# A re-planned two-layer kernel: gate row by products, a quarter scaled on ScalarE, early setups, and other distances in the planner

## The chip, the cores and the metric

One core of a Trainium2 chip runs the whole program in one launch. The metric is the device time of one execution in microseconds (us); the median of 3 runs of the kernel before is 3489.16 us (3485.51 to 3496.49). Inside the core, TensorE (PE, with its weight loads PEld), VectorE (DVE), ScalarE (ACT) and GpSimd (POOL) compute, and SyncE (SP) issues every transfer.

## What is computed

Two layers on x of 2048 rows by 1024 columns, in float32. The first layer begins with three rows of 1024 numbers, and the third of these, `gate`, is used only at the layer's end:

```
c_act = silu(c)
shift, scale, gate = split(c_act @ ada_w + ada_b, 3)      # ada_w: 1024 x 3072
h = rmsnorm(x, g_pre) * (1 + scale) + shift
proj = h @ w_in                                           # then three mixers: window attention, rwkv, gla
y = concat(attn, rwkv, gla) @ w_out
x = x + gate * rmsnorm(y, g_post)
```

The second layer normalizes x again, projects it, picks the 256 best keys of each query by a small index product, attends to them, adds a pooled branch, and merges both by gates. It needs cosines and sines of the positions, which depend on no other result.

## The kernel before

**Stages.** The 2048 rows are worked in four quarters of 512. For each quarter, `build_h` (line 792) loads rows, normalizes and transposes them, scales them into the array `raw`, and splits `raw` into a high and a low part (float32r), since each dense product is taken as three float32r products of parts (`mm3`). `dense` then runs the projections; the weights of a tile are split once by `weights` (line 895), stored as two parts of 512 KB each in an internal DRAM tensor (`scr_w`), and later loaded from there, again 512 KB a part, into a ring of two buffers for each part. Then come the mixers, the first output product, the second layer's projections, the search for the best keys and the attention, and the second output (`out2`).

**The start.** `body` (line 2209) records `setup`, the early rows of quarter 0, `ada` (shift and scale), `split_early`, the first dense tiles of quarter 0, `build_h` of quarter 1, `ada_gate` (line 771), `setup2` (line 1696: cosines and sines, and some scaled columns), `pool_setup` (line 2084: a few constants by 64 one-column MEMSETs on VectorE), then `proj1_setup`, whose product `d_wx` three of the tiles need. `ada_gate` makes the row `gate` in two halves (j = 4 and 5). For each half `ada_rows` (line 760) loads eight pieces of 128x512 of `ada_w` and accumulates them on VectorE, one TENSOR_SCALAR and seven SCALAR_TENSOR_TENSOR; one product with a column of ones then adds over the partitions. The scratch row `d_grow` receives the result. The loads rotate through eight buffers.

**Scaling.** For quarter q the letter `BX[q]` (line 37) says where `build_h` applies scale and shift to the 16 transposed pieces of 128x256 that lie in PSUM: "d" records a TENSOR_SCALAR on VectorE, "a" an ACTIVATE Identity on ScalarE. The splitting copy that follows is ScalarE's either way, and the subtraction GpSimd's.

**The order of the work.** No instruction is issued when it is written. Every operation is first recorded with its dependencies and a price from a formula (`price`, line 567), and `order` (line 381) plans the whole program: `forward` (line 312) walks through time and gives each engine, whenever it is free, the ready operation of the highest rank; `backward` (line 352) computes new ranks from the plan's end; and so on for up to `PASSES` = 32 passes, ending earlier after 12 without a better plan. The plan with the lowest planned total is emitted (`emit`, line 408; so all instructions carry line 414), and each engine then runs its own list in that order, waiting at each instruction for what it needs. Three things of the planner matter here:

- Operations that may run elsewhere (`others`, line 496) have several ways: copies and scalings by a constant or a column can go to VectorE, ScalarE, and in part GpSimd. A TENSOR_SCALAR with scale and shift, both columns, has no other way; an ACTIVATE Identity with a bias may also become one on VectorE.
- `lag` (line 610) is the time between the end of one operation and the start of one that depends on it. For whatever a transfer is followed by, a load, a store that frees a buffer, or a store that a load reads back, it is 900 ns. The transfer itself is planned as an issue, 1125 ns, and its bytes at 360 per ns in one queue.
- `until` (line 291) makes VectorE and GpSimd exclude each other in the plan. A VectorE operation takes part if `port` (line 545) says so: those with two tensors in SBUF do. Copies and scalings of one tensor don't.

```
    def until(self, o, e, t):
        if e == "vector" and o.port:
            return max(t, self.held["gpsimd"] - 60.0)
        if e == "gpsimd":
            return max(t, self.held["vector"] - 60.0)
        return t
```

Of the kernel before, what the change touches and what calls it, by code (L numbers as in the profile page):

```python
# [8 lines left out]
F32 = mybir.dt.float32  # L9
F32R = mybir.dt.float32r  # L10
# [8 lines left out]
PSUM = bass.MemoryType.PSUM  # L19
# [14 lines left out]
F, S0, S2 = 0, 8, 12  # L34
W1, W2, W3, W4, W5 = 1, 1, 1, 1, 1
P1, P2, P3, P4, P5, P6 = 1, 1, 1, 1, 1, 1
BX, BY = "-dad", "ssss"
EJ = ((2, "vector"), (3, "tensor"), (0, "tensor"), (1, "vector"))
B1, B2, B3, B4, B5 = 1, 1, 1, 1, 1
K0, K1, K2, K3, M0, M1 = 3, 4, 4, 4, 2, 2  # L40
PASSES, PATIENCE = 32, 12
SWITCH, NEAR, LOOK, WAIT, AHEAD = 90.0, 3000.0, 12, 150.0, 60000.0
FLEX, MARGIN, GAIN = 3, -10000.0, 500.0
ENGINES = ("tensor", "vector", "scalar", "gpsimd", "sync")
RW, PHL, GS = 2, 4, 2

# [10 lines left out]


class Op:
    __slots__ = ("eng", "name", "args", "kw", "preds", "succs", "cost", "start", "end", "more", "ways", "kind", "port")  # L60


class Plan:
# [3 lines left out]
    def __init__(self, tc, ctx):  # L67
        self.tc, self.nc = tc, tc.nc
        self.ops = []
        self.memo = {}  # L70
        self.pitch = {}
        self.used = {}
        self.free = [(0, self.SBUF * 4)]
        self.places, self.start = {}, {}
        ps = ctx.enter_context(tc.tile_pool(name="psum", bufs=1, space=PSUM))
        self.banks = [ps.tile([128, 512], F32, name=f"bank{i}") for i in range(8)]
        self.bank_names = {b.name: i for i, b in enumerate(self.banks)}
        self.idle = list(range(8))
        self.rings = {}
        self.junk = ()  # L80
        self.totals = []
        for e in ("tensor", "vector", "scalar", "gpsimd", "sync"):
            setattr(self, e, Engine(self, e))
# [98 lines left out]
    def record(self, eng, name, args, kw):  # L182
        o = Op()
        o.eng, o.name, o.args, o.kw = eng, name, args, kw
        o.preds, o.succs, o.more = {}, [], set()
        i = len(self.ops)
        reads, writes = operands(name, args, kw)
        o.cost = price(eng, name, args, kw, reads, writes)
        o.ways = [(eng, name, args, kw, o.cost)]
        o.kind = kind(name, reads) if eng == "tensor" else None  # L190
        o.port = port(name, reads)
        for way in others(eng, name, args, kw, reads, writes):
            o.ways.append((*way, price(*way, reads, writes)))
        for aps, w in ((reads, False), (writes, True)):
            for ap in aps:
                r = self.region(ap)
                if r is not None:
                    self.touch(o, i, r, w and ap.tensor.name not in self.junk, ap.tensor.name)
        o.preds.pop(i, None)
        self.ops.append(o)  # L200
# [89 lines left out]

    def until(self, o, e, t):

        if e == "vector" and o.port:
            return max(t, self.held["gpsimd"] - 60.0)
        if e == "gpsimd":
            return max(t, self.held["vector"] - 60.0)
        return t
# [14 lines left out]
    def forward(self, rank, goal):  # L312

        ops = self.ops
        end, seq, dma = [0.0] * len(ops), [], [0.0]

        def take(i, e, t, now, avail, done):
            o = ops[i]
            free = self.until(o, e, t)
            if len(o.ways) > 1:  # L320
                mine = next(w for w in o.ways if w[0] == e)
                home = o.ways[0][0]
                if e != home:
                    slack = goal - rank[i] - t + MARGIN
                    if slack > 0:
                        return t + slack
                    w = o.ways[0]
                    start = max(now[home], t)
                    start += sum(ops[j].cost for r, j in avail[home] if -r > rank[i] and not done[j])
                    if start + w[4] <= t + mine[4] + GAIN:  # L330
                        return max(start + w[4] - mine[4] - GAIN, t + 50.0)
                o.eng, o.name, o.args, o.kw, o.cost = mine
            o.start = t
            if e == "sync":
                now[e] = t + 475
                dma[0] = o.end = max(dma[0], t + 1125) + o.cost
            else:
                now[e] = o.end = free + o.cost
                if o.port and e in self.held:
                    self.held[e] = o.end  # L340
                if e == "tensor":
                    if o.kind != self.kind:
                        now[e] = o.end = o.end + SWITCH
                    self.kind = o.kind
            end[i] = o.end
            seq.append(i)

        self.walk([len(o.preds) for o in ops],
                  lambda i: [(s, end[i] + lag(ops[i], ops[s], data)) for s, data in ops[i].succs], rank, take)
        return max(end), end, seq  # L350

    def backward(self, end):

        ops = self.ops
        tail, dma = [0.0] * len(ops), [0.0]
        ways = [o.ways for o in ops]
        for o in ops:
            o.ways = [(o.eng, o.name, o.args, o.kw, o.cost)]

        def take(i, e, t, now, avail, done):  # L360
            o = ops[i]
            if e == "sync":
                now[e] = t + 475
                dma[0] = max(dma[0], t) + o.cost
                tail[i] = dma[0] + 1125
            else:
                now[e] = tail[i] = self.until(o, e, t) + o.cost
                if o.port and e in self.held:
                    self.held[e] = tail[i]
                if e == "tensor":  # L370
                    if o.kind != self.kind:
                        now[e] = tail[i] = tail[i] + SWITCH
                    self.kind = o.kind

        self.walk([len(o.succs) for o in ops],
                  lambda i: [(p, tail[i] + lag(ops[p], ops[i], data)) for p, data in ops[i].preds.items()], end, take)
        for o, w in zip(ops, ways):
            o.ways = w
        return tail

    def order(self):

        ops = self.ops
        for i, o in enumerate(ops):
            for j, data in o.preds.items():
                ops[j].succs.append((i, data))
        rank = [0.0] * len(ops)
        for i in reversed(range(len(ops))):
            rank[i] = max((rank[s] + lag(ops[i], ops[s], data) for s, data in ops[i].succs), default=0.0) + ops[i].cost
        best, goal = None, math.inf  # L390
        stale = 0
        for k in range(PASSES):
            total, end, seq = self.forward(rank, goal)
            stale += 1
            if stale > PATIENCE:
                break
            if best is None or total < best[0]:
                stale = 0
                best = total, seq, [(o.eng, o.name, o.args, o.kw, o.cost, o.start, o.end) for o in ops]
            rank = self.backward(end)  # L400
            goal = total
            self.totals.append(total)
        self.total, self.seq, how = best
        for o, h in zip(ops, how):
            o.eng, o.name, o.args, o.kw, o.cost, o.start, o.end = h
        return self.seq
# [135 lines left out]
         "copy_predicated", "tensor_tensor_reduce"}  # L542


def port(name, reads):

    if name not in PAIRS:
        return False
    return all(reads[i].space != PSUM for i in (0, -1 if name == "scalar_tensor_tensor" else 1))


# [8 lines left out]
def width(ap):  # L560
    n = 1
    for d in list(ap.shape)[1:]:
        n *= d
    return n
# [45 lines left out]
def lag(a, b, data):  # L610

    if a.eng == b.eng and not data:
        return 0.0
    if a.eng == "sync":
        return 900.0
    if b.eng == "sync":
        return 100.0
    return LAG[a.eng][b.eng]
# [6 lines left out]
class Kern:  # L625
# [145 lines left out]
    def ada_gate(self):  # L771
        nc, A = self.nc, self.A
        for j in (4, 5):
            acc = self.ada_rows(j)
            p = self.bank("mt", NT)[:1]
            nc.tensor.matmul(p, self.ones1, acc, start=True, stop=True)
            r = self.x0.tile([1, 512], F32, name="adar", bufs=2)
            nc.sync.dma_start(r, dram(A["ada_b"], j * 512, [[0, 1], [1, 512]]))
            g = self.x0.tile([1, 512], F32, name="adag", bufs=2)
# [1429 lines left out]
def body(tc, A):  # L2209
    with ExitStack() as ctx:  # L2210
        K = Kern(tc, A, ctx)
        tc = K.plan
# [12 lines left out]
        with tc.tile_pool(name="c1", bufs=1) as K.c1:  # L2225
            with tc.tile_pool(name="x0", bufs=1, top=True) as K.x0:
# [6 lines left out]
                dense(t1[:M0], "x", (0,))  # L2233
                build("x", 1)
                K.ada_gate()
                K.setup2()
                K.pool_setup()
            K.proj1_setup()
            K.rwkv_setup()
            K.gla_setup()  # L2240
# [95 lines left out]
```

## Time and profile before

| | |
|---|---|
| median of 3 runs | 3489.16 us (3485.51 to 3496.49) |
| the profiled execution: its own time | 3483.89 us |
| its span, first to last instruction | 3482.1 us |
| mean granted TensorE clock, share of full speed | 0.956 |
| instructions | 53683 |
| busy: PE, PEld, DVE, ACT, POOL | 91%, 74%, 69%, 50%, 38% |
| moved by transfers | 631.69 MB, mean 181 GB/s |

The span is the time between the first and the last instruction of the profiled execution; 1.8 us of its own time lie around it. Busy shares are averages over stages with different limits. In rows of waits the columns are the engine, what it waited for, the total in us, the number of waits and the longest. In rows of groups the columns are busy us, mean ns of one, and the idle time before. In rows of the timeline they are the start, the length, the engine and the operation, and in brackets the idle time before and what ended it. "x4" counts instructions, and a float32 product appears as two MATMUL records. The clock column of the windows is the granted TensorE clock as a share of 2.4 GHz, so 0.50 is 1.2 GHz.

### The profile page before, as it was taken

Reading aid. Unit: us, or ns where it says so; the run is one execution under the profiler, and the core shown is the slowest. Engines: PE = TensorE matmul, PEld = TensorE weight load, DVE = VectorE, ACT = ScalarE, POOL = GpSimd, SP = SyncE. Lnnn points to the kernel's source line nnn. Section 1 sums busy time; section 2 is a strip of 40 time slices with the busy share of each in tenths; the row PEclk is TensorE's granted clock in tenths of the full one; section 3 lists DMA queues with packets and bytes.
Section 4 is the critical chain, followed back from the end, with each engine's and each line's share of the span. In section 5 each row is a group of like instructions: output and inputs, shape, how many; then the busy total and the mean of one; then the engine's idle time right before and its main releaser. Section 6 shows DMA issues by size and latency. Waiting matters only on the chain.

```text
span 3482.1 us, 53683 instructions
## 1 busy us (share of the span) xinstructions
PE 3165.3 (91%) x18258; PEld 2567.1 (74%) x18258; DVE 2399.1 (69%) x5421; ACT 1756.7 (50%) x3458; POOL 1336.7 (38%) x1379
## 2 busy tenths in 40 slices
PE   6899988998898999798999999999999988898988
PEld 5677666776666888787887777777777766777877
DVE  6367966666883656258878888789788687775442
ACT  3122225432123454257776767875786957446330
POOL 2232545441333554443323444353132236353421
PEclk7899989999998999999999999999999999899999
DMA  8477467547547888656644344362322346665656
GB/s 273 170 248 209 157 174 229 167 151 214 150 121 232 256 271 296 214 173 216 212 157 137 134 139 140 132 213 91 120 73 90 121 152 230 226 212 163 212 162 220
DMA packets 453961, 631.69 MB, mean 181 GB/s; under 512 B 83751, under 2 KB 309552, under 8 KB 453430
## 3 DMA queue, kind: packets, MB, share of 16 engines
q1 hardware_dynamic: 453686, 628.26, 56.1%
q8 instruction: 143, 2.34, 0.3%
q14 instruction: 132, 1.08, 0.1%
HBM read 397.31 MB, written 230.82 MB: 180 GB/s over the span
## 4 chain that ended last, share of the span: by engine, by line
PE 38%; DMA 13%; DVE 9%; ACT 6%; issue 4%; POOL 3%; SPq 1%; ACTq 0%; DVEq 0%; POOLq 0%
PE bank L414 38%; DVE arena L414 9%; DMA arena<-scr_w 6%; ACT arena L414 6%; POOL arena L414 3%; DMA arena<-in_w_in 1%; DMA arena<-in_w_out 1%; DMA out<-arena 1%; SPq L414 1%; DMA arena<-scr_y 0%; DMA arena<-scr_q 0%; DMA scr_x<-arena 0%; DMA arena<-scr_p_zb 0%; DMA arena<-in_w_branch_b 0%; DMA arena<-scr_yT 0%
## 5 line engine op out<-in xcount | busy, mean ns | idle before, releaser
L414 PE MATMUL bank<-arena 128*128 128x512 f32 (+8 forms) x18258 | 3165.3, 337 | 312.5 <-DVE arena L414 124.4
L414 PEld LDWEIGHTS bank<-arena 128*128 128x128 f32 (+3 forms) x18258 | 2567.1, 181 | 910.4 <-DVE arena L414 225.2
L414 POOL TENSOR_TENSOR arena<-arena 128x512 fp32r<-128x512 f32 (+16 forms) x1116 | 1240.1, 1127 | 1618.8 <-ACT arena L414 975.3
L414 ACT ACTIVATE arena<-arena 128x512 fp32r<-128x512 f32 (+32 forms) x1195 | 966.7, 824 | 804.4 <-DVE arena L414 421.1
L414 ACT ACTIVATE arena<-bank 128x512 f32<-128x512 f32 (+8 forms) x1423 | 724.4, 550 | 797.6 <-PE bank L414 649.9
L414 DVE TENSOR_TENSOR arena<-arena 128x512 fp32r<-128x512 f32 (+27 forms) x822 | 583.4, 724 | 209.3 <-ACT arena L414 103.6
L414 DVE SCALAR_TENSOR_TENSOR arena<-arena 128x512 f32<-128x512 f32 (+10 forms) x661 | 433.8, 661 | 59.5 <-POOL arena L414 19.3
L414 DVE TENSOR_SCALAR arena<-arena 128x1 f32<-128x1 f32 (+6 forms) x1129 | 272.8, 248 | 168.3 <-ACT arena L414 124.9
L414 DVE TENSOR_SCALAR_CACHE_REDUCE arena<-arena 128x384 int8<-128x384 bf16 (+13 forms) x238 | 351.3, 1476 | 11.9 <-ACT arena L414 6.8
L414 DVE CUSTOM_DVE_ANT_0 arena<-bank,arena 128x512 f32<-128x512 f32 (+3 forms) x448 | 251.7, 565 | 62.6 <-PE bank L414 60.6
L414 DVE TENSOR_TENSOR arena<-bank,arena 128x512 f32<-128x512 f32 (+3 forms) x170 | 95.4, 569 | 181.2 <-PE bank L414 144.3
L414 POOL TENSOR_SCALAR arena<-arena 128x4 f32<-128x4 f32 (+10 forms) x169 | 69.0, 409 | 327.9 <-DVE arena L414 159.1
L414 DVE SCALAR_TENSOR_TENSOR arena<-arena,bank 128x512 f32<-128x512 f32 (+1 forms) x264 | 127.5, 487 | 75.6 <-PE bank L414 42.4
L414 DVE COPY arena<-bank 128x512 f32<-128x512 f32 (+8 forms) x146 | 79.6, 548 | 114.9 <-PE bank L414 106.5
L414 ACT ACTIVATE arena<-bank,arena 128x512 f32<-128x512 f32 (+3 forms) x175 | 99.5, 579 | 65.0 <-PE bank L414 64.2
L414 DVE SCALAR_TENSOR_TENSOR arena<-bank,arena 64x64 f32<-64x64 f32 (+4 forms) x209 | 82.0, 393 | 63.1 <-PE bank L414 48.3
L414 ACT ACTIVATION_READ_ACCUMULATOR arena<-arena 128x1 f32 x590 | 114.9, 195 | 0.0
L414 POOL MEMSET arena<- 64x256 f32 (+7 forms) x69 | 21.8, 319 | 109.9 <-PE bank L414 57.6
L414 DVE CAST arena<-arena 128x512 fp32r<-128x512 f32 (+5 forms) x50 | 37.2, 751 | 24.2 <-PE bank L414 6.3
L414 DVE TENSOR_SCALAR arena<-bank 64x256 f32<-64x256 f32 (+2 forms) x44 | 18.0, 410 | 51.4 <-PE bank L414 47.0
L414 DVE TENSOR_TENSOR_SCAN arena<-arena 128x512 f32<-128x512 f32 (+14 forms) x26 | 53.1, 2041 | 0.2
L414 DVE TENSOR_REDUCE arena<-arena 128x1 f32<-128x3 f32 (+6 forms) x148 | 37.3, 252 | 9.5 <-ACT arena L414 8.1
(18 smaller groups left out, 215.7 us busy)
## 6 DMA issues: line engine op xcount, KB each, us to landing
arena<-scr_w SPq DMA_DIRECT2D x340, 512.0 KB
scr_w<-arena SPq DMA_DIRECT2D x174, 512.0 KB
arena<-in_w_in SPq DMA_DIRECT2D x52, 512.0 KB
arena<-in_x SPq DMA_DIRECT2D x32, 512.0 KB
scr_p_g<-arena SPq DMA_DIRECT2D x64, 256.0 KB
arena<-scr_p_g SPq DMA_DIRECT2D x64, 256.0 KB
arena<-in_ada_w SPq DMA_DIRECT2D x48, 256.0 KB
arena<-scr_p SPq DMA_DIRECT2D x16, 532.0 KB
```

Of the source, the lines that this page charges most:

```text
L414: ins = getattr(getattr(self.nc, o.eng), o.name)(*o.args, **o.kw)
```

## The change

1. `ada_gate` no longer accumulates on VectorE. Each half of the gate is a sum of eight products on TensorE, with one column of `cact` as the stationary operand and a loaded piece of 128x512 as the moving one. The loads, the addition of the bias and the product with `norm_post` stay.
2. `BX[1]` becomes "a": quarter 1 is recorded with ACTIVATE Identity.
3. Operations recorded by `setup2` and `pool_setup` are marked early, and each pass adds 60 us to their rank.
4. `lag` after a transfer becomes 2700 ns in place of 900.
5. `port` is asked for each engine, and for VectorE it now also says yes to a TENSOR_SCALAR or copy of float32 from SBUF to SBUF with more than one column and a single output.
6. Up to 200 passes, ending after 30 without a better plan.

```diff
-BX, BY = "-dad", "ssss"
+BX, BY = "-aad", "ssss"
-PASSES, PATIENCE = 32, 12
+PASSES, PATIENCE = 200, 30
+EARLY = 60000.0
...
-        o.port = port(name, reads)
+        o.early = self.early
+        o.port = {e: port(e, name, reads, writes) for e in ("vector", "gpsimd")}
...
-        if e == "vector" and o.port:
+        if e == "vector" and o.port[e]:
...
-                if o.port and e in self.held:
+                if e in self.held and o.port[e]:
...
         for k in range(PASSES):
+            rank = [r + EARLY if o.early else r for r, o in zip(rank, ops)]
             total, end, seq = self.forward(rank, goal)
...
-def port(name, reads):
+def port(eng, name, reads, writes):
     if name not in PAIRS:
-        return False
+        return eng == "vector" and name in ("tensor_scalar", "tensor_copy") and len(writes) == 1 and width(writes[0]) > 1 \
+            and all(x.space != PSUM and x.dtype in (F32, F32R) for x in reads[:1] + writes)
...
     if a.eng == "sync":
-        return 900.0
+        return 2700.0
...
     def ada_gate(self):
         for j in (4, 5):
-            acc = self.ada_rows(j)
             p = self.bank("mt", NT)[:1]
-            nc.tensor.matmul(p, self.ones1, acc, start=True, stop=True)
+            for k in range(8):
+                nc.tensor.matmul(p, self.cact[:, k:k + 1], self.ada_load(j, k, "v"), start=k == 0, stop=k == 7)
...
                 K.ada_gate()
+                tc.early = True
                 K.setup2()
                 K.pool_setup()
+                tc.early = False
```

Since `order` plans all operations together, every one of these edits can move any instruction of the program on any engine's list.

## Rows read from the trace of the kernel before

**Rows 1.** Windows of four stretches: PE, PEld, DVE, ACT, POOL busy, PEclk, DMA share, GB/s.

```profile
0.00:1044.00 1044.00, 927.68 (x4977) 712.11 (x4978) 709.02 (x1534) 309.73 (x692) 384.46 (x360) 0.93 0.61 189
1044.00:1740.00 696.00, 614.57 (x4397) 544.57 (x4397) 412.63 (x1159) 359.77 (x951) 301.45 (x361) 0.94 0.72 234
1740.00:2786.00 1046.00, 1014.02 (x5337) 802.71 (x5336) 853.04 (x1987) 772.21 (x1353) 386.81 (x448) 0.99 0.39 129
2786.00:3482.00 696.00, 608.99 (x3551) 507.69 (x3549) 424.40 (x746) 314.97 (x463) 263.98 (x210) 0.96 0.60 197
```

**Rows 2.** Waits over the whole span, of PE and of the transfers' queue (SPq).

```profile
PE bank L414 <- DVE arena L414: 124.4, 107, 10.1
PE bank L414 <- ACT arena L414: 78.6, 76, 6.1
PE bank L414 <- DMA arena<-scr_w: 73.7, 52, 11.0
...
SPq L414 <- PE bank L414: 900.4, 376, 20.3
```

**Rows 3.** Waits of PE for scr_w, in the four stretches of rows 1.

```profile
PE bank L414 <- DMA arena<-scr_w: 18.2, 12, 4.9
...
PE bank L414 <- DMA arena<-scr_w: 31.6, 15, 11.0
...
PE bank L414 <- DMA arena<-scr_w: 4.7, 7, 1.2
...
PE bank L414 <- DMA arena<-scr_w: 19.2, 18, 2.4
```

**Rows 4.** Windows of the start, columns as in rows 1.

```profile
47.00:60.00 13.00, 3.70 (x10) 2.24 (x11) 12.56 (x16) 5.80 (x10) 9.06 (x6) 0.50 0.85 265
60.00:83.00 23.00, 18.75 (x83) 13.64 (x82) 20.87 (x43) 6.70 (x13) 10.11 (x8) 0.87 0.76 238
83.00:101.00 18.00, 6.81 (x18) 3.28 (x18) 17.40 (x43) 2.78 (x6) 4.32 (x6) 0.50 0.61 201
...
117.00:174.00 57.00, 54.75 (x226) 43.46 (x226) 6.85 (x14) 10.69 (x14) 12.16 (x6) 0.94 0.55 191
```

**Rows 5.** Groups of VectorE by shape, from 47 to 101 us.

```profile
L414 DVE SCALAR_TENSOR_TENSOR arena<-arena 128x512 f32<-128x512 f32 x14 | 10.3, 739 | 0.0
...
L414 DVE TENSOR_SCALAR arena<-bank,arena 128x256 f32<-128x256 f32 x16 | 7.7, 532 | 0.5 <-PE bank L414 0.4
...
L414 DVE SCALAR_TENSOR_TENSOR arena<-arena 128x128 f32<-128x128 f32 x9 | 2.5, 283 | 0.1
```

**Rows 6.** The product with a one-column stationary operand: timeline, and its group to 130 us.

```profile
89.48 1.87 PE L414 MATMUL bank<-arena 128*1 128x512 f32 x2 [5.26 <-DVE arena L414]
...
L414 PE MATMUL bank<-arena 128*1 128x512 f32 x4 | 2.9, 814 | 5.3 <-DVE arena L414 5.3
```

**Rows 7.** Groups of ScalarE over the span: Identity with columns for scale and bias.

```profile
L414 ACT ACTIVATE arena<-bank,arena 128x256 f32<-128x256 f32 x40 | 19.6, 514 | 16.2 <-PE bank L414 16.2
```

**Rows 8.** Loads: a 512 KB one in the timeline, a pair of 512 KB in the chain.

```profile
109.07 0.38 SPq L414 DMA_DIRECT2D arena<-in_w_in  x1
...
113.21 1.06 ACT L414 ACTIVATE arena<-arena 128x1024 fp32r<-128x1024 f32 x1 [3.54 <-DMA arena<-in_w_in]
...
3082.64 7.29 DMA arena<-scr_w
```

**Rows 9.** Timeline of the start: VectorE scalings of 128x1024, and a GpSimd subtraction.

```profile
20.41 1.41 DVE L414 TENSOR_SCALAR arena<-arena 128x1024 f32<-128x1024 f32 x2 [7.43 <-POOL arena L414]
...
51.31 7.09 POOL L414 TENSOR_TENSOR arena<-arena 128x1024 fp32r<-128x1024 f32 x3 [0.68 <-ACT arena L414]
...
54.45 5.41 DVE L414 TENSOR_SCALAR arena<-arena 128x1024 f32<-128x1024 f32 x4
```

**Rows 10.** Timeline: the last MEMSETs of the setups, and the load of the positions.

```profile
12.60 0.38 DVE L414 MEMSET arena<- 128x1 f32 x24
...
44.39 1.65 SPq L414 DMA_DIRECT2D arena<-in_positions  x1
```

More of the change, by code (lines that the diff above doesn't have):

```diff
@@ L59 @@
 class Op:
-    __slots__ = ("eng", "name", "args", "kw", "preds", "succs", "cost", "start", "end", "more", "ways", "kind", "port")
+    __slots__ = ("eng", "name", "args", "kw", "preds", "succs", "cost", "start", "end", "more", "ways", "kind", "port", "early")
 class Plan:
@@ L80, in __init__ @@
         self.junk = ()
+        self.early = False
         self.totals = []
@@ L367, in take @@
                 now[e] = tail[i] = self.until(o, e, t) + o.cost
-                if o.port and e in self.held:
+                if e in self.held and o.port[e]:
                     self.held[e] = tail[i]
```

## The prediction

> **What bounds the kernel.** I read the page's shares first, where TensorE leads with 91%, and then the windows: its busy time is 927.7 + 614.6 + 1014.0 + 609.0 = 3165 us of 3482 [rows 1], so some 317 us are left in which it does nothing, and what the change can win lies in them unless it takes work off TensorE, which it does not. The same windows say where that time is: 116.3 us before 1044, 81.4 to 1740, 32.0 to 2786 and 87.0 in the last stretch [rows 1]. The third stretch has TensorE busy 97% of the time, so the other three carry what can be had. The waits name the causes: TensorE waited 124.4 us for VectorE, 78.6 for ScalarE and 73.7, in 52 waits, for loads of split weights from scr_w [rows 2]. By stretch, those loads are 18.2, 31.6, 4.7 and 19.2 us [rows 3]: few where TensorE has much other work, long where it has not. Last I read the start in finer windows. From 47 to 101 us VectorE is busy 12.56 + 20.87 + 17.40 = 50.8 of 54 us, and TensorE 3.70 + 18.75 + 6.81 = 29.3, with a granted clock of 0.50, its lower level of 1.2 GHz, in the first and the last of these windows, where it had little to do [rows 4]. Here VectorE is the bound. From 117 to 174 us TensorE is busy 54.75 of 57 [rows 4], so what the start saves moves all that follows forward.
>
> **Gate row and second quarter, together.** Both take work off VectorE just in that stretch. The gate's accumulations are 14 SCALAR_TENSOR_TENSOR of 0.739 us, 10.3 us busy [rows 5], and two first TENSOR_SCALARs, which I count at the same price, 1.5 us at most. Quarter 1 has 16 scalings of 0.532 us, 7.7 us busy [rows 5]. VectorE is left with 50.8 - 10.3 - 1.5 - 7.7 = 31.3 us. ScalarE takes the 16 at 0.514 us each [rows 7], 8.2 us; it is busy 15.3 of the 54 us [rows 4], so this lies beside other work, and without that cover it would cost at most the 8.2. The planner may hand an Identity back to VectorE; then VectorE has 39.0 us, which is still below what TensorE needs, so I cost that at nothing.
>
> TensorE pays. One product with a one-column stationary operand took 1.87 us at the lower clock, and the two of them 4 x 0.814 = 3.26 us, so the other took 1.39 [rows 6]. Sixteen come and two go: 14 x 1.39 = 19.5 us at the price of the second, 14 x 1.87 = 26.2 at that of the first, and 14 x 0.94 = 13.1 if all ran at the upper clock and the price is halved with it. TensorE then has 42.4 to 55.5 us of work in a stretch of 54. I take the middle price, since the clock in this stretch is between its levels: 48.8 us, a gain of **5 us**, between 12 and a loss of 1. The loads of the gate stay as they are, in number and in SP's queue; only their reader changes, and a late one now holds up TensorE's list behind it instead of VectorE's.
>
> **Small setups first.** The 64 MEMSETs run by 13 us already [rows 10], when VectorE has nothing else to do. What really moves is the cosine chain, which begins with the load of the positions, issued at 44.39 us [rows 10]: some 25 small operations on VectorE, 9 of which took 0.283 us each [rows 5]; at that price they are 7 us in all. They cost the same wherever they stand; ahead of the scalings that open quarter 0 they would delay these by at most 7 us, and behind them by nothing. I take 0, because VectorE has just been relieved of 19 us there, and keep 0 and 7. One more load goes ahead in SP's queue, 1.65 us by its row [rows 10].
>
> **Loads counted longer.** A 512 KB load is planned as 1.125 + 524288/360000 = 2.58 us, plus 0.9: 3.48 us before, 5.28 after. A pair in one queue is 4.94 before and 6.74 after. In the trace the single load took from 109.07 to 113.21, 4.14 us, and a pair in the last stretch 7.29 [rows 8]. So the plan of before was short by 0.66 and 2.35 us, and the new one is over by 1.14 and short by 0.55. Where the plan is short, TensorE's list reaches a product whose weights aren't there, and stands. Where it is over, the list has other work first and the load is early, which costs nothing on TensorE. The 45 waits outside the third stretch come to 69.0 us, 1.53 each; the 7 inside it, where other products stand ready, to 4.7, or 0.67 each [rows 3]. If the 45 came down to 0.67, that would be 45 x 0.86 = 38.7 us. I take a third of it, **13 us**: an instruction put forward into a gap has inputs too, and TensorE's 203 us of waits for VectorE and ScalarE [rows 2] say that these are often what is late next. The bounds are all 73.7 us, and a loss of 16, an estimate: a fifth of the 78.6 us of waits for ScalarE added by a new order.
>
> The other answer to the same question comes from the Trainium skill. Its page "DMA: Bandwidth & Descriptors", section "Anatomy of one DMA — SWDGE (gpsimd) path", gives, for transfers that GpSimd issues, about 2.0 us fixed plus the bytes at 436 GB/s, which makes an estimate of 3.2 us for 512 KB: by that rule 3.48 was already enough, the load term is 0 and the time 3482 us. The trace speaks against it with 4.14 and 7.29 us.
>
> **Copies exclude GpSimd.** Two VectorE scalings of 128x1024 took 1.41 us without GpSimd at work; four took 5.41 while GpSimd ran a subtraction of 7.09 us in three [rows 9]. That is 2.6 us more than 4 x 0.70, in the stretch that VectorE bounds. Counting this lets the planner put something else there. I take **2 us**; the bounds are 2.6 and a loss of 2.4, one subtraction of 7.09 / 3 that now starts later with a product behind it. Elsewhere VectorE is not the bound.
>
> **More passes.** No row shows what a plan's lower total is worth on the chip; I take 0, and its two sides lie within those of the load term, which is also a matter of order.
>
> **The sum.** 5 + 13 + 2 = 20 us. The profiled execution took 3483.9 us, which gives 3463.9; the median of the runs is 5.3 us above it, so I predict **3469 us** as a median.
>
> **Rivals.**
> - *The load waits are waits for buffers.* The rings hold two buffers for each part, and the transfers' queue stood 900.4 us waiting for TensorE [rows 2]: a load that can't be issued sooner isn't helped by an earlier place. For it: 45 of the 52 waits are in stretches with little else to do. Against: 49.8 us of these waits are in the first and second stretch, where other tiles are open. Only 5 + 2 us are won: 3489 - 7 = 3482 us. Chance 0.12.
> - *The loads were counted long enough.* Then the 0.66 us by which the single load exceeded the plan was chance, and the new distance changes order without effect: again 3482 us. Against it is the pair of 7.29 us. Chance 0.08. The rule of the skill's page above would give this one.
> - *The products fill TensorE at the start* (slower). TensorE has 24.7 us idle from 47 to 101, and at the lower clock the products ask for 26.2. If half of its old waits stay, 12.4 us, because its list is in order and now also stands for pieces of `ada_w`, the stretch takes 29.3 + 26.2 + 12.4 = 67.9 us, 13.9 more than 54. Without a gain at the loads that is 3503 us. It decides once more than 54 - 55.5 + 10.5 = 9 us of TensorE's idle time remain there, a loss beyond what can be told apart. For it: the clock of 0.50 in two of three windows. Against: the gate is needed late, so the planner can place products in gaps. Chance 0.20.
> - *The loads give all of it*, the 38.7 us, and the start 12 and 3: 54 us, 3435 us. For it: the plan's shortage of 2.35 us at a pair is of the size of the waits. Chance 0.15.
> - My forecast has the rest, 0.45.
>
> **Range and chances.** A measurement of this kernel tells about 0.3% from no change, 10.5 us. Faster by more than that are my forecast and the last rival, 0.60; within it the two with 3482 us, 0.20; slower the products, 0.20. The range goes from the last rival's 3435 to 3502, just under the slower rival's own time, which leaves out about a tenth at each end.
>
> **What would show it.** Right: from 47 us on, the stretch up to where TensorE becomes busy without a break ends some 5 us earlier; there are no SCALAR_TENSOR_TENSOR of 128x512 for the gate and 32 or so more records with a one-column operand, at 0.7 to 0.9 us each; the waits of PE for scr_w fall from 73.7 to about 60 us or lower, mainly in the first two stretches, and PE's idle time from 317 to just under 300. Wrong: the start ends later than before, with PE waiting for in_ada_w; or the scr_w waits fall and those for VectorE or ScalarE rise by as much; or PE's own busy time grows by more than 20 us.

## The result, and the profile after

The changed kernel takes 3384.03 us (median of 4 runs, 3382.6 to 3389.28) beside 3492.82 us for the kernel before in the same session: a ratio of 0.9688, 95% interval [0.9657, 0.9719]. That is 109 us faster where 20 were forecast, and 51 us below the range. The sign was right, the size wrong by a factor of five.

The head and the first part of the page of the kernel after, then TensorE's waits over the span, then the span and mean clock of the core:

```profile
span 3380.8 us, 53657 instructions
...
PE 3134.4 (93%) x18286; PEld 2549.5 (75%) x18286; DVE 2352.6 (70%) x5364; ACT 1770.4 (52%) x3491; POOL 1349.3 (40%) x1387
```

```profile
PE bank L418 <- DVE arena L418: 106.5, 96, 11.5
PE bank L418 <- ACT arena L418: 70.8, 67, 13.0
...
PE bank L418 <- DMA arena<-scr_w: 20.0, 18, 2.7
```

```profile
core 0: 3380.8 us, clock 0.968
```

The span fell by 101.3 us. TensorE's idle time went from 3482.1 - 3165.3 = 316.8 to 3380.8 - 3134.4 = 246.4, so 70.4 us of it is idle time; the other 30.9 are busy time, though 28 records more are carried out. Its waits for scr_w went from 73.7 us in 52 waits [rows 2] to 20.0 in 18. The waits for VectorE and ScalarE, which I had expected to take the place of those won, fell too, from 203 to 177 us.

Where along the run it was won is read from windows cut at the same events in both kernels: the first store of scr_yT, the first load of scr_grow, the last store of scr_y, the last store of scr_p_za, the first store of out. Columns as in rows 1. Before:

```profile
0.00:412.00 412.00, 351.49 (x1685) 277.22 (x1686) 264.70 (x534) 105.69 (x172) 131.36 (x116) 0.91 0.67 217
412.00:1148.30 736.30, 664.34 (x3745) 502.68 (x3745) 483.69 (x1121) 239.02 (x618) 290.33 (x277) 0.94 0.60 178
1148.30:1685.70 537.40, 478.88 (x3602) 433.30 (x3603) 327.29 (x909) 280.06 (x751) 248.17 (x299) 0.95 0.72 235
1685.70:2425.30 739.60, 710.44 (x3916) 570.75 (x3915) 618.89 (x1513) 536.28 (x1003) 300.93 (x343) 0.99 0.45 151
2425.30:2970.40 545.10, 512.52 (x2582) 400.91 (x2581) 430.19 (x891) 397.40 (x625) 193.29 (x216) 0.98 0.40 132
2970.40:3482.10 511.70, 447.59 (x2736) 382.22 (x2734) 274.33 (x462) 198.23 (x293) 172.62 (x130) 0.95 0.60 199
```

And after:

```profile
0.00:417.80 417.80, 374.29 (x1767) 287.21 (x1768) 246.40 (x509) 120.68 (x199) 128.12 (x116) 0.93 0.69 219
417.80:1117.80 700.00, 636.17 (x3673) 487.30 (x3672) 471.99 (x1105) 235.08 (x607) 287.30 (x274) 0.95 0.62 183
1117.80:1632.70 514.90, 470.12 (x3587) 424.74 (x3587) 322.06 (x871) 275.03 (x741) 243.10 (x294) 0.97 0.76 245
1632.70:2358.10 725.40, 701.55 (x3884) 566.03 (x3883) 603.26 (x1485) 537.94 (x1014) 299.49 (x342) 1.00 0.45 153
2358.10:2886.00 527.90, 510.51 (x2626) 403.36 (x2624) 426.83 (x900) 380.41 (x611) 195.57 (x217) 0.99 0.42 137
2886.00:3380.80 494.80, 441.71 (x2758) 380.81 (x2756) 282.04 (x499) 221.26 (x324) 195.72 (x147) 0.96 0.64 207
```

The first stretch gained nothing, it is 5.8 us longer; the others gave 36.3, 22.5, 14.2, 17.2 and 16.9 us. So it is not one place. Even the two stretches from 1685.7 to 2970.4, which hold most of what I had set aside as 97% busy, gave 31 us. The counts of records differ too (1767 for 1685 in the first stretch, 3673 for 3745 in the second): work of TensorE went from one stretch to another.

The chain of waits over nearly the same last part shows what ends last there, by engine and transfer, first before (from 1800 us on), then after (from 1750 on):

```profile
by line: PE bank L414 56.5%; DVE arena L414 9.6%; ACT arena L414 8.3%; DMA arena<-scr_w 7.7%; issue 5.7%; POOL arena L414 4.0%; DMA out<-arena 1.5%; DMA arena<-in_w_out 1.2%; DMA arena<-in_w_in 0.9%; DMA arena<-scr_p_zb 0.7%; DMA arena<-in_
```

```profile
by line: PE bank L418 52.4%; DVE arena L418 19.3%; ACT arena L418 10.4%; issue 7.4%; POOL arena L418 3.8%; DMA arena<-scr_w 2.1%; DMA out<-arena 1.5%; DMA arena<-scr_p_g 1.1%; DMA arena<-scr_h 0.4%; SPq L418 0.4%; DMA arena<-scr_p_zb 0.4%; 
```

The loads of split weights leave this chain, 7.7% to 2.1%, and VectorE comes in, 9.6% to 19.3%.

### The profile page after: what moved, and what is told of

Same layout as the page of the kernel before. It is cut to its first block, busy times and chain, and to the rows that moved or that the text cites. A ratio compares the mean times of both kernels' runs of the same rounds, so it can differ in the third digit from the quotient of the medians.

```text
span 3380.8 us, 53657 instructions
## 1 busy us (share of the span) xinstructions
PE 3134.4 (93%) x18286; PEld 2549.5 (75%) x18286; DVE 2352.6 (70%) x5364; ACT 1770.4 (52%) x3491; POOL 1349.3 (40%) x1387
## 3 DMA queue, kind: packets, MB, share of 16 engines
q14 instruction: 132, 1.08, 0.1%
## 5 line engine op out<-in xcount | busy, mean ns | idle before, releaser
L418 PE MATMUL bank<-arena 128*128 128x512 f32 (+9 forms) x18286 | 3134.4, 335 | 242.4 <-DVE arena L418 106.5
L418 PEld LDWEIGHTS bank<-arena 128*128 128x128 f32 (+5 forms) x18286 | 2549.5, 180 | 827.1 <-DVE arena L418 182.9
L418 POOL TENSOR_TENSOR arena<-arena 128x512 fp32r<-128x512 f32 (+14 forms) x1125 | 1262.7, 1140 | 1512.6 <-ACT arena L418 792.9
L418 ACT ACTIVATE arena<-arena 128x512 fp32r<-128x512 f32 (+28 forms) x1208 | 980.0, 828 | 713.5 <-DVE arena L418 453.5
L418 ACT ACTIVATE arena<-bank 128x512 f32<-128x512 f32 (+7 forms) x1424 | 722.8, 549 | 775.4 <-PE bank L418 654.4
L418 DVE TENSOR_TENSOR arena<-arena 128x512 fp32r<-128x512 f32 (+26 forms) x813 | 583.3, 730 | 184.2 <-ACT arena L418 85.8
L418 DVE SCALAR_TENSOR_TENSOR arena<-arena 128x512 f32<-128x512 f32 (+6 forms) x647 | 426.5, 663 | 35.8 <-ACT arena L418 12.3
L418 DVE TENSOR_SCALAR arena<-arena 128x1 f32<-128x1 f32 (+7 forms) x1114 | 253.3, 234 | 192.5 <-ACT arena L418 150.0
L418 POOL TENSOR_SCALAR arena<-arena 128x4 f32<-128x4 f32 (+9 forms) x168 | 59.1, 352 | 323.5 <-DVE arena L418 165.2
L418 DVE COPY arena<-bank 128x512 f32<-128x512 f32 (+7 forms) x148 | 79.9, 544 | 152.0 <-PE bank L418 127.2
L418 DVE CAST arena<-bank 128x512 fp32r<-128x512 f32 (+3 forms) x50 | 29.8, 598 | 13.9 <-PE bank L418 8.5
```

The costliest lines, as they stand in the source:

```text
L418: ins = getattr(getattr(self.nc, o.eng), o.name)(*o.args, **o.kw)
```

## The experiments

The main theory was that the longer distance after a transfer is nearly all of it; the rivals were the port's rule, and a sum of many small parts. Then: which transfers it acts through, and how far two orders that mean the same differ. All ratios are to the kernel before, timed beside each.

### The distance and the port's rule, alone and left out

```diff
     if a.eng == "sync":
-        return 900.0
+        return 2700.0
```

> The kernel before with one edit: a transfer's followers are counted 2700 ns after it, in place of 900. Theory (the longer distance is nearly all of it): about 3400 us (0.97 to 0.98 of before), TensorE's waits for scr_w down from 73.7 us to 30 or lower, its idle time from 317 us to 260 or lower. Rival (VectorE copies that exclude GpSimd are the main part): 3470 us or more, within 0.5% of before, though the waits for scr_w fall. Rival (the sum of many small parts, a third of them this): some 3455 us.

Measured: 3367.42 us, 0.9637 [0.9609, 0.9665]. This one line gives all that the change gave. The busy times of its page, TensorE's waits, and its span and clock:

```profile
PE 3118.2 (93%) x18258; PEld 2549.4 (76%) x18258; DVE 2371.1 (71%) x5419; ACT 1755.7 (52%) x3470; POOL 1364.4 (41%) x1369
```

```profile
PE bank L414 <- DVE arena L414: 118.1, 108, 11.3
PE bank L414 <- ACT arena L414: 60.8, 74, 4.2
...
PE bank L414 <- DMA arena<-scr_w: 24.1, 18, 2.9
```

```profile
core 0: 3359.5 us, clock 0.970
```

With the same 18258 records as before, idle time fell by 75.5 us (316.8 to 241.3) and busy time by 47.1. The busy times of the page before:

```profile
PE 3165.3 (91%) x18258; PEld 2567.1 (74%) x18258; DVE 2399.1 (69%) x5421; ACT 1756.7 (50%) x3458; POOL 1336.7 (38%) x1379
```

The other way round, the changed kernel with `return 900.0`:

> The changed kernel with the distance put back to 900 ns. Theory (the longer distance): 3470 to 3490 us, the waits for scr_w back at about 70 us. Rival (the port's rule): at most 3410 us. Rival (small parts): some 3425 us.

Measured: 3477.24 us, 0.9950 [0.9924, 0.9975], with 66.6 us of TensorE's waits for scr_w. All the other parts together are worth half a per cent, no more than two orders that mean the same differ by (0.4 to 0.7%, shown below).

```diff
     if name not in PAIRS:
-        return eng == "vector" and name in ("tensor_scalar", "tensor_copy") and len(writes) == 1 and width(writes[0]) > 1 \
-            and all(x.space != PSUM and x.dtype in (F32, F32R) for x in reads[:1] + writes)
+        return False
```

> The changed kernel in which VectorE's copies and scalings don't take part in the exclusion, as before. Theory (the longer distance): 3375 to 3400 us, within 0.5% of the changed kernel. Rival (the port's rule): 3450 us or more. Rival (small parts): 3400 to 3430 us.

Measured: 3365.30 us, 0.9638 [0.9614, 0.9663]: without the port's rule the changed kernel is no slower.

> The kernel before with one edit: VectorE's copies and scalings of float32 within SBUF exclude GpSimd in the plan. Theory (the longer distance): 3475 to 3500 us, no change to speak of. Rival (the port's rule): 3430 us or less. Rival (small parts): 3450 to 3470 us.

Measured (the kernel before with the new `port` and nothing else): 3473.23 us, 0.9940 [0.9919, 0.9962]. So the rule gives 0.6% by itself, which can't be told from another order, and nothing beside the distance. The rivals of the port and of many small parts fall.

### Which followers of a transfer

```diff
-        return 900.0
+        return 2700.0 if data and b.eng != "sync" else 900.0    # e5: a load's data, to a computing engine
+        return 2700.0 if not data else 900.0                    # e6: a store's buffer, overwritten
+        return 2700.0 if data and b.eng == "sync" else 900.0    # e7: a store's value, loaded back
+        return 2700.0 if data and b.eng == "tensor" else 900.0  # e9: a load's data, to TensorE
```

> The kernel before; 2700 ns only from a load to the computing engine's operation that uses its data, all else 900. Theory A (the gain comes from loads that a computing engine finds late): 3380 to 3410 us, the waits of TensorE for scr_w at 30 us or lower. Theory B (from stores, whose buffers were planned free too early): 3470 us or more. Theory C (from values stored and loaded back, whose second transfer was planned too early): 3450 us or more.

> The kernel before; 2700 ns only from a store to the operation that overwrites the buffer which it read. Theory A (late loads): 3480 to 3500 us. Theory B (buffers planned free too early): 3420 us or less. Theory C (values stored and loaded back): 3480 to 3500 us.

> The kernel before; 2700 ns only from a store to the load that reads its value back, and between transfers otherwise. Theory A (late loads): 3470 to 3500 us. Theory B (buffers): 3480 to 3500 us. Theory C (values stored and loaded back): 3430 us or less.

> The kernel before; 2700 ns only from a load to TensorE's product that uses it. If the gain is TensorE standing at its own weights: most of what loads alone gave, 3400 to 3425 us. If it lies in the loads that ScalarE, VectorE and GpSimd wait for (raw weights to be split, rows, stored tiles), and TensorE only feels it through them: 3450 us or more.

Measured: e5 3407.33 us, 0.9772 [0.9743, 0.9800]; e6 3487.00 us, 0.9987 [0.9973, 1.0001]; e7 3481.57 us, 0.9980 [0.9965, 0.9994]; e9 3442.14 us, 0.9836 [0.9795, 0.9877]. Loads are the larger part. TensorE's own loads gave 1.6 of their 2.3%, and e9 fell between the two ranges that I had given; the 0.6% between e5 and e9 is no more than the scatter of orders. Buffers and round trips alone give next to nothing. The kinds don't add up: 2.3 + 0.1 + 0.2 = 2.6%, and together 3.6%. Whether that is a true joint effect isn't settled: the missing 1.0% is less than twice the scatter of orders below. What e9 left standing is ScalarE's wait for transfers: its total was 272 us in e9, 271 before and 169 in e1 (all of ScalarE's rows with a transfer added up). The largest of these rows is that for raw weights, here of the kernel before, of e9, of e1 and of the kernel after:

```profile
ACT arena L414 <- DMA arena<-in_w_in: 92.4, 26, 13.1
```

```profile
ACT arena L414 <- DMA arena<-in_w_in: 127.4, 35, 13.3
```

```profile
ACT arena L414 <- DMA arena<-in_w_in: 60.6, 19, 6.4
```

```profile
ACT arena L418 <- DMA arena<-in_w_in: 65.3, 19, 12.0
```

TensorE's waits in e9 show what became of the waits that were won:

```profile
PE bank L414 <- DVE arena L414: 142.3, 122, 11.3
PE bank L414 <- ACT arena L414: 73.4, 64, 5.9
PE bank L414 <- POOL arena L414: 39.7, 50, 3.8
PE bank L414 <- DMA arena<-scr_w: 20.6, 16, 3.7
```

Those for scr_w fell by 53.1 us, as far as in e1. But those for VectorE rose by 17.9 us and those for GpSimd by 13.5, and TensorE's idle time fell by 19.3 only (316.8 to 3443.4 - 3145.9 = 297.5): other inputs were late next. With the longer distance for all followers, in e1, they were not.

### How far, and how much is the luck of an order

The kernel before with other distances (`return 1800.0` and so on):

> The kernel before with 1800 ns for all followers of a transfer. If the gain follows how far the plan was short (0.66 us at the single load, 2.35 at the pair), 900 ns more gives somewhat over half of it: 3410 to 3440 us. If any change of distance gives it by a lucky order: anywhere from 3367 to 3500 us, with the waits for scr_w unchanged at 60 to 75 us. If only the whole 1800 ns helps: 3470 us or more.

> The kernel before with 2600 ns in place of 2700: a neighbour, to see how far orders that mean the same differ. If orders differ little: 3360 to 3378 us. If by a per cent or more: outside 3345 to 3390 us, and then no single part below one per cent can be told from luck.

> The kernel before with 2800 ns. A second neighbour of 2700 (3367 us) beside 2600 (3385 us). If orders scatter by half a per cent around a level: 3355 to 3390 us. If the size of the distance matters within 100 ns: under 3355 us.

> The kernel before with 3600 ns. If being over costs nothing: 3350 to 3385 us, the waits of TensorE for scr_w at 20 us or lower. If too long a distance makes the plan leave gaps that weren't needed, or hold back what is ready: 3395 us or more.

> The kernel before with 950 ns, a neighbour of 900. If orders scatter by half a per cent: 3475 to 3510 us. If the kernel before had an unlucky order among its like: 3470 us or less.

| distance, ns | us | ratio [95% interval] | TensorE's waits for scr_w, us |
|---|---|---|---|
| 900 (before) | 3492 to 3499 in six sessions | 1 | 73.7 |
| 950 | 3467.78 | 0.9930 [0.9903, 0.9957] | 57.9 |
| 1800 | 3422.27 | 0.9801 [0.9778, 0.9823] | 32.8 |
| 2600 | 3384.92 | 0.9674 [0.9637, 0.9712] | 21.3 |
| 2700 | 3367.42 | 0.9637 [0.9609, 0.9665] | 24.1 |
| 2800 | 3381.56 | 0.9689 [0.9667, 0.9711] | 23.2 |
| 3600 | 3399.65 | 0.9739 [0.9723, 0.9756] | 24.6 |

Two readings. A step of 50 or 100 ns, which means nothing by itself, moves the time by 0.4 to 0.7%: the whole program's order is new each time, and that is how well a single plan can be told from its like. The time at 950 is what was expected if the kernel before had an unlucky order, so 0.7 of the 3.6% may be that; 2600 fell between its two ranges. And over this scatter there is a trend: some 2.6% from 950 to the three at 2600 to 2800, half of it at 1800, where the waits are halved too. At 3600 the time is longer than at all three, by 0.5 to 1.0%, though TensorE's waits for scr_w are as low. Its waits of the whole span there, the three largest for engines and that one:

```profile
PE bank L414 <- DVE arena L414: 101.4, 100, 11.5
PE bank L414 <- ACT arena L414: 88.9, 103, 4.8
PE bank L414 <- POOL arena L414: 34.0, 43, 3.7
PE bank L414 <- DMA arena<-scr_w: 24.6, 9, 8.8
```

The waits for ScalarE are 88.9 us against 60.8 in e1, but those for VectorE are lower, 101.4 against 118.1, and TensorE's idle time, 3393.7 - 3132.2 = 261.5 us, is that at 2800, 3382.8 - 3120.3 = 262.5. So the waits don't explain why 3600 takes longer than 2800. The size is near the scatter: that counting too long costs something is possible, not shown.

### The other parts

> The kernel before with the longer distance and the port's rule, none of the other parts. If the port's rule costs what lies between the changed kernel and that without the rule, some 17 us: 3375 to 3392 us. If that difference is the luck of one order: 3355 to 3374 us.

Measured (distance and port's rule): 3370.77 us, 0.9633 [0.9590, 0.9676], the same as the distance alone. The 17 us between the changed kernel and e3 are of the size of the scatter of orders; no cost of the rule is shown.

The gate row by products and quarter 1 on ScalarE (the two edits of the change, on the kernel before), at four distances:

> The kernel before with the gate row by products and quarter 1 on ScalarE, nothing else. My step of 5 us: 3480 to 3492 us, VectorE's busy time from 47 to 101 us down by 15 to 20 us, TensorE's up by 13 to 26. If the products fill TensorE at the start: 3500 us or more.

> The kernel before with the longer distance, the gate row by products and quarter 1 on ScalarE. If the gate's 42 us are a steady effect and add: 3325 to 3345 us. If only the 5 to 12 us of its stretch are: 3352 to 3375 us. If nothing of it holds beside the distance: 3367 to 3390 us.

> The kernel before with 950 ns, the gate row by products and quarter 1 on ScalarE; without these two it took 3468 us. If they are worth some 40 us: 3420 to 3435 us. If the 5 to 12 us of their stretch: 3450 to 3465 us, and with the scatter of orders anywhere from 3440 to 3475.

> The kernel before with 2600 ns, the gate row by products and quarter 1 on ScalarE; without these two it took 3385 us. If they are worth some 40 us: 3340 to 3350 us. If the 5 to 12 us of their stretch: 3370 to 3382 us, and with the scatter of orders anywhere from 3360 to 3390.

| distance, ns | without | with | first store of scr_yT, without and with |
|---|---|---|---|
| 900 | 1 | 3457.09 us, 0.9881 [0.9843, 0.9918] | 412.0, 409.6 us |
| 950 | 0.9930 | 3460.48 us, 0.9912 [0.9881, 0.9943] | 398.4, 403.4 us |
| 2600 | 0.9674 | 3388.63 us, 0.9696 [0.9646, 0.9745] | 426.3, 417.7 us |
| 2700 | 0.9637 | 3355.20 us, 0.9615 [0.9597, 0.9632] | 414.7, 405.9 us |

One pair alone would have said 42 us. The four pairs say -1.2, -0.2, +0.2 and -0.2%, and the event that ends the first stretch, the first store of scr_yT, moves by -2.4, +5.0, -8.6 and -8.8 us, 3.7 us earlier on the mean. The ratios' mean, -0.3%, isn't clear of the scatter of orders. Nearly all of the first pair's 42 us came after 412 us, and no other pair repeats them: another order is the likely cause.

e13, at 3355.20 us the fastest of all, beats both kernels: the distance with the gate and the quarter, without the port's rule, the early setups and the passes. It is 0.7% ahead of the changed kernel (0.9615 against 0.9688) and 0.2% ahead of e1, and by the scatter above neither says that its parts are the better ones. The early setups and the passes by themselves weren't tried; e2 holds them, with all the rest, at half a per cent.

## Why the prediction was wrong

**What bounds the kernel: half right.** Waits of TensorE for loads of split weights were named as the thing to win. Setting the third stretch aside because TensorE is 97% busy in it was wrong: in e1 the two stretches between 1685.7 and 2970.4 us took 719.1 + 512.9 = 1232.0 us instead of 1284.7, 53 us of its 122.6, and the second stretch (412 to 1148 us before) 675.0 instead of 736.3:

```profile
414.70:1089.70 675.00, 618.05 (x3608) 473.24 (x3607) 469.30 (x1095) 222.76 (x577) 269.11 (x251) 0.96 0.64 187
...
1625.50:2344.60 719.10, 698.13 (x3894) 568.02 (x3894) 606.41 (x1478) 533.97 (x1005) 284.69 (x317) 1.00 0.46 155
2344.60:2857.50 512.90, 493.57 (x2523) 392.45 (x2522) 392.97 (x809) 355.01 (x577) 191.61 (x195) 0.99 0.42 139
```

A stretch isn't short by its own waits alone: these take 137, 22 and 59 records fewer than the same stretches before, because TensorE did that work in the other stretches, which take 220 more.

**The step that failed: the load term.** I took "a third of" 38.7 us, 13 us; the distance alone measured 122.6 us of span, beyond even the bound of 73.7. The mechanism, a plan that is short and lists that stand for loads, was the one described; the size failed in three parts.
- The third. In e1 the waits for scr_w fell by 49.6 us, more than my full 38.7, and no other wait took their place. Where TensorE's own loads alone were counted longer, in e9, others did: of 53.1 us, 19.3 were won in idle time, about the third that I took. So, with one order's scatter on it, the third fits the one row that I priced, but not the edit that was made, which counts every engine's loads longer.
- Only one row was priced. I counted TensorE's waits for scr_w. ScalarE, VectorE and GpSimd waited for transfers too, 271, 132 and 163 us before and 169, 100 and 118 in e1, all their rows added up, and TensorE's waits for ScalarE fell from 78.6 [rows 2] to 60.8. That these fell because ScalarE's own loads came earlier is argued. e9 against e1 says that TensorE's own loads are some half of the gain or less: 1.6 of 3.6%, each with the scatter of orders on it. The sum over all engines is no price either: in the kernel after, GpSimd's waits for transfers were 226 us, more than before, and the time fell all the same.
- Busy time had no term. It fell by 47.1 us for the same records, and by 19.4 in e9. The clock accounts for much of it in e1: from the traces' records of the clock, TensorE was busy for 243.1 us at 1.2 GHz before and for 153.3 in e1, and 89.8 us less at half speed are up to 45 us, by estimate. But the run at 1800 ns has the clock of the kernel before, 0.956, and 235.9 us busy at 1.2 GHz, and its busy time is still 23.5 us lower:

```profile
PE 3141.8 (92%) x18258; PEld 2570.0 (75%) x18258; DVE 2398.4 (70%) x5467; ACT 1745.9 (51%) x3440; POOL 1328.1 (39%) x1351
```
So the clock isn't all of it, and what else is stays open. Nor is the profiled pair typical: beside the experiments the kernel before ran at clocks from 0.951 to 0.967, the middle one 0.961, and e1 at 0.964 to 0.970.

**Over is free: not confirmed.** At 3600 ns the time is 3399.65 us, above those at 2600 to 2800, by no more than about the scatter.

**Gate row and second quarter: the work about as forecast, the gain not shown.** The start after, columns as in rows 4, and then the group of the one-column products up to 180 us:

```profile
47.00:60.00 13.00, 6.43 (x19) 4.10 (x20) 11.33 (x18) 6.96 (x11) 8.21 (x6) 0.50 0.97 306
60.00:83.00 23.00, 23.00 (x95) 12.44 (x94) 11.67 (x22) 15.09 (x27) 11.88 (x11) 0.97 0.74 217
83.00:101.00 18.00, 13.40 (x32) 3.38 (x31) 11.89 (x39) 4.55 (x10) 2.03 (x3) 0.75 0.47 169
```

```profile
L418 PE MATMUL bank<-arena 128*1 128x512 f32 x32 | 19.1, 708 | 1.8 <-DMA arena<-in_ada_w 1.8
```

VectorE has 34.9 us where 50.8 were and 31.3 were forecast; TensorE 42.8 where 29.3 were and 48.8 were forecast; the products took 2 x 0.708 = 1.42 us each, the middle price. But the sign that was to show the gain, an earlier end of the start, isn't there in the changed kernel. These are the records with which TensorE's busy stretch from about 117 us on begins, before (a view up to 132 us) and after (up to 125 us):

```profile
116.76 15.48 PE L414 MATMUL bank<-arena 128*128 128x512 f32 x67 [1.12 <-POOL arena L414]
```

```profile
116.44 1.20 PE L418 MATMUL bank<-arena 128*128 128x512 f32 x4 [1.75 <-ACT arena L418]
118.89 6.46 PE L418 MATMUL bank<-arena 128*128 128x512 f32 x20 [1.24 <-POOL arena L418]
```

The first stretch of the changed kernel ends 5.8 us later. The four pairs have it 3.7 us earlier on the mean, from 8.8 earlier to 5.0 later: they neither show 5 us nor exclude them.

**Small setups: 0, as taken, as far as it shows.** The load of the positions is issued at 3.02 us instead of 44.39 [rows 10], and nothing waits for it. **Copies exclude GpSimd: nothing that can be told from order.** VectorE's scalings were spared only in part: from 47 to 101 us three of 128x1024 took 0.74 us each after, where five took 1.36 before, but eight of 128x512 took 1.08, where ten took 0.71. **More passes: 0, not tried alone.**

**The rivals.** That the waits are waits for buffers falls with e1. That the loads were counted long enough falls too, with e8 and e1, since 900 ns more already gave 2%. By the page "DMA: Bandwidth & Descriptors" of the Trainium skill, section "Anatomy of one DMA — SWDGE (gpsimd) path", no load term was due; the page speaks of transfers that GpSimd issues, the measured 4.14 and 7.29 us [rows 8] are of SP's, and these decide. The slower rival, products that fill the start, had its sign, since TensorE kept 54 - 42.8 = 11.2 us idle and more than 9 were to decide for it. But it had counted 55.5 us of work beside them, where 42.8 were done, and the start didn't grow by 13.9 us; TensorE's waits for VectorE in it fell from 20.0 to 2.8 us. So that sign decided nothing. The fastest rival, 3435 us, had the right mechanism and still half the size. The forecast chance of faster, 0.60, was on the right side.

## What to carry to other kernels

Where one planner orders the whole program, a distance that is counted too short can cost at every place where it occurs, on every engine. The bottleneck's own row of waits, 73.7 us here, is then no upper bound: the span fell by 122.6. The sum over all engines isn't the price either, so try the one constant alone before the finer parts. Measure the distance in the trace (issue to first use, alone and in pairs) and put it into the plan before anything finer is tuned. And before a part of half a per cent is believed, time neighbours that mean the same: here they differ by 0.4 to 0.7%, and a single pair gave a small part 42 us that three other pairs don't show.

## What was unexpected

TensorE's busy time isn't fixed by its work: the same 18258 records took 3165.3 us before and 3118.2 in e1, with mean granted clocks of 0.956 and 0.970, and 3141.8 at 1800 ns, with 0.956 again. And two stretches that were 96 and 94% busy (710.44 of 739.60, 512.52 of 545.10 us) still became 53 us shorter in e1. An estimate of 15 us of these is work done elsewhere: 81 records fewer, at the 0.19 us that one takes there on the mean.
